# Expert loop of a two-block model: TensorE's order tied to the program, down products one expert later, return products two later

## The chip, the cores and the metric

The kernel runs on one core of one Trainium2 chip. The metric is the time of one execution on the device in microseconds; shown is the median of three runs. A profile of one further execution comes with it.

## What is computed

The program is a two-block model of 256 tokens with width 1024: a mixer and a memory attention, then a mixture of experts, then a second block of feed-forward parts, a recurrence and an attention. The change touches the mixture of experts alone. Each token goes to the two best of 32 experts, and an expert is a gated unit with three matrices:

```python
def hierarchical_moe(h, w_route_group, b_route_group, w_route_expert, b_route_expert,
                     w_gate, w_up, w_down):
    t = h.reshape(-1, D)                                  # 256 tokens x 1024
    ...                                                   # top-1 group, top-2 experts in it
    gates = jnp.sum(jax.nn.one_hot(ids, N_EXPERTS) * w[..., None], axis=1)
    gates = gates.astype(h.dtype).T                       # 32 x 256, two non-zero per token

    def expert_step(y, args):
        wg, wu, wd, ge = args                             # 1024x512, 1024x512, 512x1024
        out = (jax.nn.silu(t @ wg) * (t @ wu)) @ wd
        return y + ge[:, None] * out, None

    y, _ = lax.scan(expert_step, jnp.zeros_like(t), (w_gate, w_up, w_down, gates))
    return y.reshape(B, S, D)
```

All of it is in float32; the weights of the 32 experts are 192 MiB, and each is read once.

## The kernel before

An expert works on 64 slots (`CAP`) instead of 256 tokens. Eight steps belong to one expert e, in `experts` (L772) and its helpers:

- **Gather** (L807, matmuls at L815): a one-hot matrix `oh` brings the tokens' columns into slots, in two halves `tokh` and `tokl`. It is done for a group of four experts at a time, a quarter per expert, while the group before is worked on; the result goes from a PSUM bank of ring "B" into the tiles `gx`, two copies by VectorE (L821) and two by ScalarE (L819).
- **Slots** (L823): two matmuls turn `oh` around (L828), ScalarE copies the result to `oT` (L830); two more fetch the slots' gate and norm factor (L833), VectorE adds them to `gt` (L835). The two results stand in two banks of ring "B".
- **Gate/up product** (`expert_in`, L872, matmuls at L879): four weight tiles t = 0 to 3 of 1024 KB; gate and up stand in the upper and lower half of a bank of ring "A".
- **gu** (L856): ScalarE scales that bank into `gu`.
- **Transposes** (`expert_act`, L882, L887): four, into a bank of ring "A"; then `sl` by ScalarE (Silu, L889) and `hx` by VectorE (L891).
- **Down product** (`expert_down`, L894, L903): two weight tiles, into a bank of ring "B"; then `yh` by ScalarE (L906) and `yl` by VectorE (L907), high and low part of the gated result.
- **Return product** (`combine`, L910, L917): 16 matmuls take `yh` and `yl` with `oT` back to tokens and add them into four PSUM banks `acc` that stay for the whole loop.

A matmul here has 64 columns of output partitions in the gate/up and down products (two stand side by side in the array), 128 in the gather, slots and transposes, and 64 rows in the return product. A float32 matmul of a weight tile shows as two records in the trace, so a weight tile is 8 records.

In the program, iteration e writes: the first two gate/up tiles of e, the down product of e-1, the last two gate/up tiles of e, gu, a quarter of the next group's gather, the slots of e+1, the return product of e-1, the transposes and hx of e. The order on the engines is not that of the program: a scheduler places each engine's instructions by its own estimate of when they can start, so pieces move against each other. After expert 5 stands a branch (`rest`, L764 to L767) that all engines take: only if an expert had more than 64 tokens is its body run. The scheduler works on the part ahead of the branch and the part behind it separately.

Weight tiles are loaded by SyncE's queue (`wraw`, L160), in order, into 12 buffers: six named `raw`, three `wh`, three `wl`, taken in turn as wh, raw, wl, raw. A load waits until the tile twelve back has been used. The tiles of the last expert all go into `raw`, because `wh` and `wl` hold split weights of the next part, the feed-forward part (its tiles come from `ffn_w`, its splits are at L156 and L157, its matmuls at L171 to L173). PSUM rings "A" and "B" have two banks each, `acc` four.

Of the kernel before, what the change touches and what calls it, by code (L numbers as in the profile page):

```python
# [8 lines left out]
F32 = mybir.dt.float32  # L9
F32R = mybir.dt.float32r  # L10
# [3 lines left out]
AX = mybir.AxisListType  # L14
PSUM = bass.MemoryType.PSUM

P = 128
T = 256
D = 1024
# [3 lines left out]
NE = 32  # L23
CAP = 64
# [23 lines left out]
class Block:  # L48
    def __init__(s, ctx, tc, io):
        s.tc, s.nc, s.ctx, s.io = tc, tc.nc, ctx, io  # L50
        s.n = s.turn = s.place = 0
        pool = lambda name, bufs, **k: ctx.enter_context(tc.tile_pool(name=name, bufs=bufs, **k))
        s.cp = pool("const", 1)
        s.wp = pool("weights", 3)
        s.tp = pool("temps", 2)
        s.xp = pool("x", 1)
        s.pa = pool("acc", 1, space=PSUM)
        s.pp = pool("ps", 2, space=PSUM)
# [713 lines left out]
    def experts(s, mt, pos, gs, rest):  # L772
        nc = s.nc
        mm = nc.tensor.matmul

        num = s.new(mt, [P, CAP], "num")
        nc.gpsimd.iota(num, pattern=[[1, CAP]], base=1, channel_multiplier=0, allow_small_or_imprecise_dtypes=True)
        idr = s.new(mt, [P, P], "idr", F32R)
        nc.scalar.copy(idr, s.ident)


        hh, hl = s.pair(mt, 2, "tok", N=D)
        for k in range(0, KC, 2):
            pt = s.ps([P, 2, 2, P])
            for j in range(2):
                xs = s.tmp([P, T])
                nc.scalar.mul(xs, s.xT[:, k + j], s.col("norm_ffn_g", k + j))
                for h in range(2):
                    nc.tensor.transpose(pt[:, h, j], xs[:, h * P:(h + 1) * P], s.ident)
            dst = slice(k * P, (k + 2) * P)  # L790
            src = pt.rearrange("p h j b -> p h (j b)")
            nc.scalar.copy(hh[:, :, dst], src)
            nc.vector.tensor_sub(hl[:, :, dst], src, hh[:, :, dst].bitcast(F32))

        def group(e0):


            n = 4
            oh = s.new(mt, [P, 2, n, 2 * CAP], "oh", F32R, 2)
            sh = [P, n, 2, CAP]  # L800
            for h in range(2):
                nc.vector.tensor_tensor(oh[:, h].rearrange("p n (a c) -> p n a c", a=2),
                                        num.unsqueeze(1).unsqueeze(1).to_broadcast(sh),
                                        pos[:, h, e0:e0 + n].unsqueeze(2).unsqueeze(3).to_broadcast(sh), op=ALU.is_equal)
            return n, oh, ([], [])

        def gather(g, k):  # L807

            n, oh, gx = g
            if not gx[k // 4]:  # L810
                gx[k // 4].extend(s.new(mt, [P, 4, CAP], "gx", F32, 12) for _ in range(n))
            pg = s.ps([P, 2, n, CAP], "B")
            for j in range(2):
                for i, (src, h) in enumerate(((hh, 0), (hh, 1), (hl, 0), (hl, 1))):
                    mm(pg[:, j], src[:, h, (k + j) * P:(k + j + 1) * P], oh[:, h, :, 0:CAP], start=i == 0, stop=i == 3)  # L815
            for i, x in enumerate(gx[k // 4]):
                dst = x[:, k % 4:k % 4 + 2]
                if i % 2:
                    nc.scalar.copy(dst, pg[:, :, i])  # L819
                else:  # L820
                    nc.vector.tensor_copy(dst, pg[:, :, i])  # L821

        def slots(g, e, i):  # L823

            oh = g[1][:, :, i]
            pt = s.ps([P, 2, P], "B")
            for h in range(2):
                mm(pt[:, h], oh[:, h], idr, start=True, stop=True)  # L828
            oT = s.new(mt, [P, 2 * P], "oT", F32R, 3)
            nc.scalar.copy(oT, pt.rearrange("p a b -> p (a b)"))  # L830
            pg = s.ps([P, 2, 2], "B")
            for h in range(2):
                mm(pg.rearrange("p a b -> p (a b)"), oh[:, h], gs[:, h, e], start=h == 0, stop=h == 1)  # L833
            gt = s.new(mt, [P, 2], "gt", F32, 4)
            nc.vector.reduce_sum(gt, pg, axis=AX.X)  # L835
            return oT, gt

        nxt = group(0)
        for k in range(0, KC, 2):
            gather(nxt, k)  # L840
        prev = None
        acc = s.accs()
        for e in range(NE):
            i = e % 4
            if i == 0:
                now = nxt
                nxt = group(e + 4) if e + 4 < NE else None
                slot = slots(now, e, 0)
# [23 lines left out]
    def expert_in(s, ps, e, gx, part):  # L872


        for t in (2 * part, 2 * part + 1):
            w = s.wraw(s.io["w_gu"][e, t], 4, 512, e == NE - 1).rearrange("p (g c) n -> p g c n", c=2)
            for c in range(2):
                for g in range(2):
                    s.nc.tensor.matmul(ps[g * CAP:(g + 1) * CAP], gx[part][:, 2 * (t % 2) + c], w[:, g, c],  # L879
                                       start=t + c == 0, stop=t == 3 and c == 1)  # L880

    def expert_act(s, mt, gu):  # L882

        nc = s.nc
        pt = s.ps([P, 4, P], "A")
        for c in range(4):
            nc.tensor.transpose(pt[:, c], gu[:, c * P:(c + 1) * P], s.ident)  # L887
        sl = s.new(mt, [P, 4, CAP], "sl")
        nc.scalar.activation(sl, pt[:, :, 0:CAP], AF.Silu)  # L889
        hx = s.new(mt, [P, 4, CAP], "hx")  # L890
        nc.vector.tensor_mul(hx, sl, pt[:, :, CAP:P])  # L891
        return hx

    def expert_down(s, mt, e, hx, oT, gt):  # L894


        nc = s.nc
        pd = s.ps([P, 512], "B")
        for t in range(2):
            w = s.wraw(s.io["w_down"][e, t], 2, D, e == NE - 1)  # L900
            for c in range(2):
                for n in range(2):
                    nc.tensor.matmul(pd[n * CAP:(n + 1) * CAP], hx[:, 2 * t + c], w[:, c, n * 512:n * 512 + 512],  # L903
                                     start=t + c == 0, stop=t + c == 2)
        yh, yl = (s.new(mt, [P, 512], n, F32R) for n in ("yh", "yl"))
        nc.scalar.mul(yh, pd, gt[:, 0:1])  # L906
        nc.vector.scalar_tensor_tensor(yl, pd, gt[:, 0:1], yh.bitcast(F32), op0=ALU.mult, op1=ALU.subtract)  # L907
        return yh, yl

    def combine(s, acc, e, y, oT):  # L910

        mm = s.nc.tensor.matmul
        for m in range(KC // 2):
            for i in range(2):
                for n in range(2):
                    r, k = slice(n * CAP, (n + 1) * CAP), 4 * n + m
                    mm(acc[k // 2][:, k % 2], y[i][r, m * P:(m + 1) * P], oT[r], start=e == 0 and i == 0 and m % 2 == 0,  # L917
                       stop=e == NE - 1 and i == 1 and m % 2 == 1)

    def moe_over(s, over, y):  # L920

# [425 lines left out]
```

## Time and profile before

| | |
|---|---|
| median of three runs | 1767.74 us (1766.97 to 1768.96) |
| the profiled execution's own time | 1765.29 us |
| its span in the profile | 1763.5 us |
| TensorE busy, share of the span | 96% |
| expert loop, first gate/up matmul to last return matmul | 256.4 to 771.9 us |
| weight tiles of the experts | 192 of 1024 KB |

The profile shows one execution. PE is TensorE's matmuls, PEld its weight loads, DVE is VectorE, ACT ScalarE, SPq SyncE's queue. A busy TensorE in this table is not one at its peak: a group of matmuls that run side by side counts as busy throughout. Times inside the loop are in microseconds from the span's start.

### The profile page before, as it was taken

To read this page: it belongs to the slowest core of one execution; us is meant where nothing else is said; L and a number is where in the kernel's file an instruction comes from. 1 tells how busy PE (TensorE), PEld (TensorE's weight loads), DVE (VectorE), ACT (ScalarE), POOL (GpSimd) and SP (SyncE) were. 2 spreads that over 40 slices of the span, in tenths; PEclk is the share of its full clock that TensorE was granted. 3 is DMA by queue.
4 is the path that set the end of the run, shared out by engine and by line. 5 is a ranking of instruction groups with operands and counts; after the bars stand their busy time and mean duration, and the time that the engine had idled before them with its cause. 6 is when DMAs were issued, how large, how long until landed. Compare 5 with 4: busy or idle time off the path is not lost.

```text
span 1763.5 us, 28035 instructions
## 1 busy us (share of the span) xinstructions
PE 1690.5 (96%) x11820; PEld 1356.1 (77%) x11820; DVE 932.2 (53%) x1643; ACT 706.3 (40%) x1140; POOL 3.5 (0%) x19
## 2 busy tenths in 40 slices
PE   8999989999999999879999999999999999999998
PEld 7879974443333333359999999999899998689998
DVE  7998651111111111057556896555856557876554
ACT  8426432111111111144444774434644445864442
POOL 0000000000000000000000000000000000000000
PEclk9999989999999999989999999999999999899999
DMA  8425359999999999775554645555455555135540
GB/s 319 164 80 184 124 204 403 373 419 415 380 391 385 389 383 395 299 259 195 192 188 135 222 152 213 191 183 177 176 187 186 192 178 181 49 122 189 191 168 25
DMA packets 60225, 408.01 MB, mean 231 GB/s; under 512 B 6592, under 2 KB 9920, under 8 KB 11456
## 3 DMA queue, kind: packets, MB, share of 16 engines
q1 hardware_dynamic: 60096, 406.18, 62.1%
q8 instruction: 94, 1.54, 0.3%
q14 instruction: 35, 0.29, 0.0%
HBM read 405.11 MB, written 1.05 MB: 230 GB/s over the span
## 4 chain that ended last, share of the span: by engine, by line
PE 74%; ACT 3%; DVE 3%; issue 1%; ACTq 0%; DVEq 0%
PE A L879 11%; PE acc L172 6%; PE acc L171 6%; PE acc L173 6%; PE B L172 6%; PE B L171 6%; PE B L903 6%; PE B L173 5%; PE A L172 5%; PE A L173 5%; PE A L171 5%; PE acc L917 2%; PE B L815 1%; ACT yh L906 1%; ACT gu L856 1%; PE A L887 1%
## 5 line engine op out<-in xcount | busy, mean ns | idle before, releaser
L156 ACT CAST wh<-raw 128x1024 fp32r<-128x1024 f32 (+2 forms) x378 | 377.9, 1033 | 425.8 <-issue 368.7
L157 DVE TENSOR_TENSOR wl<-raw,wh 128x1024 fp32r<-128x1024 f32 (+2 forms) x378 | 448.9, 1204 | 145.3 <-ACT wh L156 144.3
L171 PE MATMUL B<-xgh,wh 128*128 128x256 f32 x872 | 246.2, 282 | 9.5 <-ACT wh L156 9.5
L171 PE MATMUL A<-xgh,wh 128*128 128x256 f32 (+1 forms) x872 | 246.0, 282 | 1.7 <-ACT xgh L215 1.7
L172 PE MATMUL A<-xgl,wh 128*128 128x256 f32 (+1 forms) x872 | 245.7, 282 | 0.3 <-DVE xgl L216 0.2
L172 PE MATMUL B<-xgl,wh 128*128 128x256 f32 x872 | 245.8, 282 | 0.0
L173 PE MATMUL B<-xgh,wl 128*128 128x256 f32 x872 | 245.6, 282 | 0.0
L173 PE MATMUL A<-xgh,wl 128*128 128x256 f32 (+1 forms) x872 | 244.9, 281 | 0.6 <-DVE wl L157 0.5
L172 PE MATMUL acc<-hl,wh 128*128 128x256 f32 x704 | 198.2, 283 | 0.2
L173 PE MATMUL acc<-hh,wl 128*128 128x256 f32 x704 | 198.2, 283 | 0.0
L171 PE MATMUL acc<-hh,wh 128*128 128x256 f32 x704 | 195.5, 282 | 0.1
L171 PEld LDWEIGHTS B<-xgh,wh 128*128 128x128 f32 x872 | 164.6, 189 | 10.7 <-ACT wh L156 10.1
L171 PEld LDWEIGHTS A<-xgh,wh 128*128 128x128 f32 (+1 forms) x872 | 164.4, 189 | 2.3 <-ACT xgh L215 1.9
L173 PEld LDWEIGHTS B<-xgh,wl 128*128 128x128 f32 x872 | 164.4, 189 | 1.5 <-DVE wl L157 1.0
L172 PEld LDWEIGHTS A<-xgl,wh 128*128 128x128 f32 (+1 forms) x872 | 164.3, 188 | 1.3 <-DVE xgl L216 1.2
L173 PEld LDWEIGHTS A<-xgh,wl 128*128 128x128 f32 (+1 forms) x872 | 164.2, 188 | 1.1 <-DVE wl L157 1.1
L172 PEld LDWEIGHTS B<-xgl,wh 128*128 128x128 f32 x872 | 164.7, 189 | 0.5 <-DVE xgl L216 0.2
L172 PEld LDWEIGHTS acc<-hl,wh 128*128 128x128 f32 x704 | 132.3, 188 | 0.6 <-DVE hl L213 0.6
L171 PEld LDWEIGHTS acc<-hh,wh 128*128 128x128 f32 x704 | 132.1, 189 | 0.8 <-ACT hh L212 0.7
L173 PEld LDWEIGHTS acc<-hh,wl 128*128 128x128 f32 x704 | 132.2, 188 | 0.0
L879 PE MATMUL A<-raw,gx 128*64 128x512 f32 x528 | 130.3, 598 | 0.0
L891 DVE TENSOR_TENSOR hx<-sl,A 128x256 f32<-128x256 f32 x32 | 13.5, 421 | 167.9 <-ACT sl L889 167.9
(404 smaller groups left out, 2449.6 us busy)
## 6 DMA issues: line engine op xcount, KB each, us to landing
raw<-in_ffn_w_dram SPq DMA_DIRECT2D x132, 1024.0 KB, 4.9
raw<-in_w_gu_dram SPq DMA_DIRECT2D x66, 1024.0 KB, 7.5
raw<-in_w_down_dram SPq DMA_DIRECT2D x33, 1024.0 KB, 8.3
wh<-in_w_gu_dram SPq DMA_DIRECT2D x31, 1024.0 KB, 7.3
wl<-in_w_gu_dram SPq DMA_DIRECT2D x31, 1024.0 KB, 7.1
wh<-in_w_down_dram SPq DMA_DIRECT2D x16, 1024.0 KB, 8.8
wl<-in_w_down_dram SPq DMA_DIRECT2D x15, 1024.0 KB, 8.9
raw<-in_a_w_in_dram SPq DMA_DIRECT2D x8, 1024.0 KB, 4.8
```

Of the source, the lines that this page charges most:

```text
L156: nc.scalar.copy(wh[:, lo:hi], raw[:, lo:hi])
L157: nc.vector.tensor_sub(wl[:, lo:hi], raw[:, lo:hi], wh[:, lo:hi].bitcast(F32))
L171: mm(out, w[0], x[0], start=first, stop=False)
L172: mm(out, w[0], x[1], start=False, stop=False)
L173: mm(out, w[1], x[0], start=False, stop=last)
L815: mm(pg[:, j], src[:, h, (k + j) * P:(k + j + 1) * P], oh[:, h, :, 0:CAP], start=i == 0, stop=i == 3)
L856: nc.scalar.mul(gu, ps, rs)
L879: s.nc.tensor.matmul(ps[g * CAP:(g + 1) * CAP], gx[part][:, 2 * (t % 2) + c], w[:, g, c], start=t + c == 0, stop=t == 3 and c == 1)
L887: nc.tensor.transpose(pt[:, c], gu[:, c * P:(c + 1) * P], s.ident)
L903: nc.tensor.matmul(pd[n * CAP:(n + 1) * CAP], hx[:, 2 * t + c], w[:, c, n * 512:n * 512 + 512], start=t + c == 0, stop=t + c == 2)
L906: nc.scalar.mul(yh, pd, gt[:, 0:1])
L917: mm(acc[k // 2][:, k % 2], y[i][r, m * P:(m + 1) * P], oT[r], start=e == 0 and i == 0 and m % 2 == 0, stop=e == NE - 1 and i == 1 and m % ...
```

## The change

TensorE's instructions in the expert loop get a fixed order: a new helper `pe` adds, from each matmul to the next one in the program, a dependency that costs no semaphore and binds the scheduler alone. It starts anew behind the branch. The program's order is rearranged: an iteration e now writes all four gate/up tiles of e, gu, the return product of e-2, a quarter of the gather, the slots of e+1, the transposes of e, and then the down product of e-1. The slots' two results share one bank, all four matmuls standing together. The down product's bank comes from ring "A" instead of "B"; `oT` gets four buffers instead of three, `hx` two instead of one. The first expert's slots come ahead of the loop; the last six weight tiles (two gate/up tiles of expert 31 and both down products of 30 and 31) go into `raw`.

```diff
+        slot = slots(nxt, 0, 0)
+        s.queue = []
+        prev = done = None
...
-            ps = s.ps([P, 512], "A")
-            s.expert_in(ps, e, gx, 0)
-            if prev is not None:
-                yy = s.expert_down(mt, *prev)
-            s.expert_in(ps, e, gx, 1)
+            ps = s.expert_in(e, gx)
             gu = s.new(mt, [P, 512], "gu", F32, 2)
             nc.scalar.mul(gu, ps, rs)
+            if done is not None:
+                s.combine(acc, *done)
             if nxt:
                 gather(nxt, 2 * i)
             own = slot
-            if i < 3 and e + 1 < NE:
-                slot = slots(now, e + 1, i + 1)
+            if e + 1 < NE:
+                slot = slots(nxt if i == 3 else now, e + 1, (i + 1) % 4)
+            hx = s.expert_act(mt, gu)
             if prev is not None:
-                s.combine(acc, e - 1, yy, prev[2])
-            hx = s.expert_act(mt, gu)
+                done = prev[0], s.expert_down(mt, *prev), prev[2]
             prev = (e, hx, *own)
             if e == 5:
                 rest()
-        yy = s.expert_down(mt, *prev)
-        s.combine(acc, NE - 1, yy, prev[2])
+                s.queue = []
+        last = prev[0], s.expert_down(mt, *prev), prev[2]
+        s.combine(acc, *done)
+        s.combine(acc, *last)
+        s.queue = None
...
+    def pe(s, ins):
+
+        if s.queue is not None:
+            if s.queue:
+                s.after(s.queue.pop(), ins)
+            s.queue.append(ins)
+        return ins
...
-        pd = s.ps([P, 512], "B")
+        pd = s.ps([P, 512], "A")
         for t in range(2):
-            w = s.wraw(s.io["w_down"][e, t], 2, D, e == NE - 1)
+            w = s.wraw(s.io["w_down"][e, t], 2, D, e >= NE - 2)
```

Every matmul of the loop is wrapped in `s.pe(...)`; `slots` puts its second result into columns 256 to 259 of the first one's bank.

TensorE in the steady loop behind the branch, expert 8, before. The names are output and inputs: `A<-wl,gx` is a gate/up tile, `B<-wh,hx` a down tile, `oh,tokh` a gather, `idr,oh` and `gs,oh` the slots, `acc<-oT,yh` a return matmul, `ident,gu` a transpose.

```order
L879 MATMUL A_3723<-wl_3724,gx_3139 64x512 x4
L879 MATMUL A_3723<-raw_3730,gx_3139 64x512 x4
L903 MATMUL B_3736<-wh_3737,hx_3708 64x512 x4
L815 MATMUL B_3771<-oh_3710,tokh_2623 128x256 x2
...
L903 MATMUL B_3736<-raw_3743,hx_3708 64x512 x4
L828 MATMUL B_3784<-idr_2621,oh_3082 128x128 x2
L917 MATMUL acc_2732<-oT_3596,yh_3749 128x256
...
L833 MATMUL B_3789<-gs_377_2611,oh_3082 128x4 x2
...
L879 MATMUL A_3723<-wl_3753,gx_3576 64x512 x4
L917 MATMUL acc_2732<-oT_3596,yl_3750 128x256
...
L879 MATMUL A_3723<-raw_3759,gx_3576 64x512 x4
L887 MATMUL A_3810<-ident,gu_3765 128x128 x4
```

And now, the same expert (the gate/up lines are L891, down L916, return L930, gather L816, slots L829 and L832, transposes L900):

```order
L891 MATMUL A_3698<-wl_3699,gx_3117 64x512 x4
L891 MATMUL A_3698<-raw_3705,gx_3117 64x512 x4
L891 MATMUL A_3698<-wh_3711,gx_3552 64x512 x4
L891 MATMUL A_3698<-raw_3717,gx_3552 64x512 x4
L930 MATMUL acc_2741<-oT_3230,yh_3691 128x256
...
L816 MATMUL B_3745<-oh_3695,tokh_2623 128x256 x2
...
L829 MATMUL B_3758<-idr_2621,oh_3071 128x128 x2
L832 MATMUL B_3758<-gs_377_2611,oh_3071 128x4 x2
L900 MATMUL A_3767<-ident,gu_3723 128x128 x4
L916 MATMUL A_3776<-wl_3777,hx_3676 64x512 x4
L916 MATMUL A_3776<-raw_3783,hx_3676 64x512 x4
```

Each kind of matmul stands in one piece; the return product stands between the gate/up product and the transposes, and the down tiles behind these.

SyncE's weight loads ahead of the branch, before:

```order
L165 DMA wl_3205<-in_w_down_dram 128x2048
L165 DMA raw_3211<-in_w_down_dram 128x2048
L165 DMA wh_3221<-in_w_gu_dram 128x2048
L165 DMA raw_3227<-in_w_gu_dram 128x2048
L165 DMA wl_3533<-in_w_gu_dram 128x2048
L165 DMA raw_3539<-in_w_gu_dram 128x2048
L165 DMA wh_3546<-in_w_down_dram 128x2048
L165 DMA raw_3552<-in_w_down_dram 128x2048
L767 COMPARE_AND_BRANCH
```

And now:

```order
L166 DMA wl_3182<-in_w_gu_dram 128x2048
L166 DMA raw_3188<-in_w_gu_dram 128x2048
L166 DMA wh_3244<-in_w_down_dram 128x2048
L166 DMA raw_3250<-in_w_down_dram 128x2048
L166 DMA wl_3510<-in_w_gu_dram 128x2048
L166 DMA raw_3516<-in_w_gu_dram 128x2048
L166 DMA wh_3522<-in_w_gu_dram 128x2048
L166 DMA raw_3528<-in_w_gu_dram 128x2048
L768 COMPARE_AND_BRANCH
```

38 loads stand ahead of the branch in both. The last four are those of iteration 6: two gate/up and two down tiles before, four gate/up tiles now.

## Rows read from the trace of the kernel before

**Rows 1.** The page, part 2: GB/s in 40 slices of 44 us.

```profile
GB/s 319 164 80 184 124 204 403 373 419 415 380 391 385 389 383 395 299 259 195 192 188 135 222 152 213 191 183 177 176 187 186 192 178 181 49 122 189 191 168 25
```

**Rows 2.** Stretches of the expert loop, with the columns' names ahead.

```profile
core 0: us, PE busy (x) PEld busy (x) DVE busy (x) ACT busy (x) POOL busy (x), PEclk, DMA share, GB/s
284.00:328.00 44.00, 43.52 (x255) 20.22 (x253) 6.86 (x17) 7.97 (x19) 0.00 (x0) 1.00 1.01 420
340.00:428.00 88.00, 79.35 (x427) 34.09 (x429) 12.72 (x32) 13.52 (x33) 0.00 (x0) 1.00 1.01 419
430.00:709.00 279.00, 257.18 (x1370) 107.85 (x1366) 36.19 (x91) 43.59 (x103) 0.00 (x0) 1.00 0.98 387
```

**Rows 3.** Waits, 250 to 790 us: who for whom, us, times, longest.

```profile
PE A L887 <- ACT gu L856: 19.7, 25, 0.8
PE acc L917 <- ACT yh L906: 14.0, 26, 0.8
PEld A L879 <- DMA raw<-in_w_down_dram: 0.9, 3, 0.3
SPq L165 <- PE A L879: 303.0, 116, 9.6
```

**Rows 4.** Timeline, one expert behind the branch: start, us, instruction, [idle before].

```profile
399.91 1.94 PE L903 MATMUL B<-raw,hx 128*64 128x512 f32 x8
...
402.69 0.50 PE L917 MATMUL acc<-oT,yh 64*128 64x256 f32 x3 [0.48 <-ACT yh L906]
...
409.25 0.66 PE L887 MATMUL A<-ident,gu 128*128 128x128 f32 x4 [0.79 <-ACT gu L856]
...
409.84 1.94 PE L879 MATMUL A<-wl,gx 128*64 128x512 f32 x8
...
410.42 0.42 DVE L891 TENSOR_TENSOR hx<-sl,A 128x256 f32<-128x256 f32 x1 [6.72 <-ACT sl L889]
...
416.28 1.94 PE L903 MATMUL B<-raw,hx 128*64 128x512 f32 x8
```

**Rows 5.** Timeline of TensorE, two experts ahead of the branch.

```profile
295.50 0.50 PE L815 MATMUL B<-oh,tokh 128*128 128x256 f32 x2
...
309.91 0.50 PE L815 MATMUL B<-oh,tokh 128*128 128x256 f32 x2
...
311.05 0.39 PE L917 MATMUL acc<-oT,yh 64*128 64x256 f32 x2
...
312.20 0.66 PE L887 MATMUL A<-ident,gu 128*128 128x128 f32 x4
...
313.13 1.94 PE L879 MATMUL A<-wl,gx 128*64 128x512 f32 x8
...
323.58 0.50 PE L815 MATMUL B<-oh,tokh 128*128 128x256 f32 x2
```

**Rows 6.** Timeline of SyncE's queue: weight loads at the refill and around the branch.

```profile
261.63 0.33 SPq L165 DMA_DIRECT2D wh<-in_w_down_dram  x1
...
272.57 0.33 SPq L165 DMA_DIRECT2D wh<-in_w_gu_dram  x1
...
320.26 0.33 SPq L165 DMA_DIRECT2D raw<-in_w_down_dram  x1
333.51 0.34 SPq L165 DMA_DIRECT2D wl<-in_w_gu_dram  x1
```

**Rows 7.** Stretches of 4 us around the branch, columns as in rows 2.

```profile
328.00:332.00 4.00, 4.00 (x22) 1.40 (x20) 0.42 (x1) 0.10 (x1) 0.00 (x0) 1.00 0.54 221
332.00:336.00 4.00, 4.00 (x22) 1.33 (x20) 0.54 (x1) 0.69 (x1) 0.00 (x0) 1.00 0.37 94
```

**Rows 8.** Timeline of TensorE at the end of the loop.

```profile
765.64 3.65 PE L903 MATMUL B<-raw,hx 128*64 128x512 f32 x16 [0.93 <-DVE hx L891]
...
771.58 0.28 PE L917 MATMUL acc<-oT,yl 64*128 64x256 f32 x2
773.54 0.58 PE L171 MATMUL A<-xgh,wh 128*128 128x256 f32 x1 [1.69 <-ACT xgh L215]
```

More of the change, by code (lines that the diff above doesn't have):

```diff
@@ L814, in gather @@
                 for i, (src, h) in enumerate(((hh, 0), (hh, 1), (hl, 0), (hl, 1))):
[L815 removed]
+                    s.pe(mm(pg[:, j], src[:, h, (k + j) * P:(k + j + 1) * P], oh[:, h, :, 0:CAP], start=i == 0, stop=i == 3))
             for i, x in enumerate(gx[k // 4]):
@@ L825, in slots @@
             oh = g[1][:, :, i]
-            pt = s.ps([P, 2, P], "B")
+            pt = s.ps([P, 512], "B")
             for h in range(2):
[L828 to L831, printed above, removed]
+                s.pe(mm(pt[:, h * P:(h + 1) * P], oh[:, h], idr, start=True, stop=True))
+            pg = pt[:, T:T + 4]
             for h in range(2):
-                mm(pg.rearrange("p a b -> p (a b)"), oh[:, h], gs[:, h, e], start=h == 0, stop=h == 1)
+                s.pe(mm(pg, oh[:, h], gs[:, h, e], start=h == 0, stop=h == 1))
+            oT = s.new(mt, [P, 2 * P], "oT", F32R, 4)
+            nc.scalar.copy(oT, pt[:, 0:T])
             gt = s.new(mt, [P, 2], "gt", F32, 4)
-            nc.vector.reduce_sum(gt, pg, axis=AX.X)
+            nc.vector.reduce_sum(gt, pg.rearrange("p (a b) -> p a b", b=2), axis=AX.X)
             return oT, gt
@@ L847, in experts @@
                 nxt = group(e + 4) if e + 4 < NE else None
-                slot = slots(now, e, 0)
             gx, rs = [x[i] for x in now[2]], slot[1][:, 1:2]
-            ps = s.ps([P, 512], "A")
-            s.expert_in(ps, e, gx, 0)
-            if prev is not None:
-                yy = s.expert_down(mt, *prev)
-            s.expert_in(ps, e, gx, 1)
+            ps = s.expert_in(e, gx)
             gu = s.new(mt, [P, 512], "gu", F32, 2)
             nc.scalar.mul(gu, ps, rs)
+            if done is not None:
+                s.combine(acc, *done)
             if nxt:
@@ L867, in experts, with expert_in @@
                 rest()
-        yy = s.expert_down(mt, *prev)
-        s.combine(acc, NE - 1, yy, prev[2])
-        return acc
-    def expert_in(s, ps, e, gx, part):
-        for t in (2 * part, 2 * part + 1):
-            w = s.wraw(s.io["w_gu"][e, t], 4, 512, e == NE - 1).rearrange("p (g c) n -> p g c n", c=2)
+                s.queue = []
+        last = prev[0], s.expert_down(mt, *prev), prev[2]
+        s.combine(acc, *done)
+        s.combine(acc, *last)
+        s.queue = None
+        return acc
+    def pe(s, ins):
[4 more added lines that the diff above has]
+        return ins
+    def expert_in(s, e, gx):
+        ps = s.ps([P, 512], "A")
+        for t in range(4):
+            w = s.wraw(s.io["w_gu"][e, t], 4, 512, e == NE - 1 and t > 1).rearrange("p (g c) n -> p g c n", c=2)
             for c in range(2):
                 for g in range(2):
-                    s.nc.tensor.matmul(ps[g * CAP:(g + 1) * CAP], gx[part][:, 2 * (t % 2) + c], w[:, g, c],
-                                       start=t + c == 0, stop=t == 3 and c == 1)
+                    s.pe(s.nc.tensor.matmul(ps[g * CAP:(g + 1) * CAP], gx[t // 2][:, 2 * (t % 2) + c], w[:, g, c],
+                                            start=t + c == 0, stop=t == 3 and c == 1))
+        return ps
     def expert_act(s, mt, gu):
@@ L897, in expert_down @@
         nc = s.nc
-        pd = s.ps([P, 512], "B")
+        pd = s.ps([P, 512], "A")
         for t in range(2):
-            w = s.wraw(s.io["w_down"][e, t], 2, D, e == NE - 1)
+            w = s.wraw(s.io["w_down"][e, t], 2, D, e >= NE - 2)
             for c in range(2):
                 for n in range(2):
-                    nc.tensor.matmul(pd[n * CAP:(n + 1) * CAP], hx[:, 2 * t + c], w[:, c, n * 512:n * 512 + 512],
-                                     start=t + c == 0, stop=t + c == 2)
+                    s.pe(nc.tensor.matmul(pd[n * CAP:(n + 1) * CAP], hx[:, 2 * t + c], w[:, c, n * 512:n * 512 + 512],
+                                          start=t + c == 0, stop=t + c == 2))
         yh, yl = (s.new(mt, [P, 512], n, F32R) for n in ("yh", "yl"))
@@ L916, in combine @@
                     r, k = slice(n * CAP, (n + 1) * CAP), 4 * n + m
-                    mm(acc[k // 2][:, k % 2], y[i][r, m * P:(m + 1) * P], oT[r], start=e == 0 and i == 0 and m % 2 == 0,
-                       stop=e == NE - 1 and i == 1 and m % 2 == 1)
+                    s.pe(mm(acc[k // 2][:, k % 2], y[i][r, m * P:(m + 1) * P], oT[r],
+                            start=e == 0 and i == 0 and m % 2 == 0, stop=e == NE - 1 and i == 1 and m % 2 == 1))
     def moe_over(s, over, y):
```

5 lines of the change are left out of this document (2 added, 3 removed).

## Prediction

> **What bounds the kernel now.** I read the slices of the page first, to find the stretch: from about 265 to 750 us the moved data stand at 180 to 420 GB/s, far above the 170 to 220 of most other slices [rows 1]. That stretch is the expert loop. Everything outside it is left alone by the change, so only this stretch is worth reading closely. Second come stretches of the loop, with what DMA moved. Two levels are to be seen [rows 2]: 420 and 419 GB/s in 284 to 328 and 340 to 428 us, with the DMA share at 1.01, and 387 GB/s from 430 to 709 us. Third, the waits show which side gives way [rows 3]. TensorE waited for a weight tile only 3 times, 0.9 us in all, while SyncE's queue stood 303.0 us waiting for TensorE to leave a buffer. So at 387 GB/s DMA is paced by TensorE: TensorE's own order is the bound, and 419 to 420 is what DMA does when buffers are free.
>
> Then one expert after the branch, row by row [rows 4]. From the second down tile of one expert (399.91) to that of the next (416.28) are 16.37 us. Inside it TensorE stands 0.48 us until ScalarE has written yh from the down product that has just ended, and 0.79 us until ScalarE has moved the gate/up product into gu. The view of waits has these 26 and 25 times [rows 3], so most of the 32 experts pass like this. Last, an expert before the branch, where the same code got another order [rows 5]: 295.50 to 309.91 is 14.41 us, 309.91 to 323.58 is 13.67 us, and the latter row by row has no wait: gather at 309.91, return products at 311.05, transposes at 312.20, then slots, six weight tiles from 313.13 to 323.58. So the same matmuls take 13.67 us when each kind stands in one piece and 16.37 when they are interleaved. Of the 2.70 us, 1.27 are the two waits; the other 1.43 I put down to changes between kinds of matmul (11 in the one, 5 in the other), an inference.
>
> **The change, part by part.** *Down one expert later, return products two later, order tied.* The steady order becomes four gate/up tiles, 16 return matmuls of expert e-2, 8 gather matmuls, 4 slot matmuls, 4 transposes, 2 down tiles of e-1. It issues the same matmuls as [rows 5] in as few pieces, so TensorE's need per expert is 13.67 us, up to 14.41 if something like the oT wait of the neighbour expert came back. I take 13.8, next to the row whose pieces are the same.
>
> Each of today's waits gets a cover. gu: ScalarE needs 0.7 us and the way there and back, and 16 return and 8 gather matmuls (1.15 us from 311.05, 1.14 us from 309.91 [rows 5], 2.3 together) stand between. yh and yl: a whole gate/up block of 4 tiles, about 6.9 us (10.45 x 4/6 [rows 5]), stands between down and its return products. hx: it is used an expert later. The slots' two parts share one PSUM bank and are issued together, so TensorE no longer waits for the copy oT between them. Each cover gone would cost what [rows 4] show, 0.5 to 0.8 us an expert.
>
> *The PSUM ring "A"* gets three tiles an expert instead of two, of two buffers: the next gate/up product takes the bank that the transposes filled, and so waits for hx. After the transposes (409.25) hx starts at 410.42 and takes 0.42 us [rows 4], 1.6 us in all; the slots' oT copy and a gx copy may stand ahead of it on ScalarE, so up to 2.5. The down tiles between are 3.5 us. Price zero, with about 1 us to spare.
>
> *The weight queue on SyncE* asks for tiles in exactly TensorE's order (four gate/up, two down). Twelve buffers stay twelve, and tile k still waits for tile k-12. The four extra tiles ahead of the branch stay four.
>
> *So what is late next is DMA.* An expert needs 6 tiles of 1024 KB, 6.29 MB; at 419.5 GB/s that is 15.0 us, 2.50 a tile. TensorE at 13.8 gains 1.2 us an expert on DMA, uses up its lead of some six tiles by about the middle of the loop, and from there on waits for every tile. The end is set by the last tile's landing. Its sum: twelve tiles land ahead of the loop; the refill starts with the issue at 261.63 [rows 6], at full rate 1.6 us later (after the issue at 333.51 [rows 6] the row 332 to 336 [rows 7] holds 94 GB/s x 4 us = 0.9 us of full rate, so it began at 335.1), at 263.2. 180 tiles x 2.50 = 450.0 us. Two holes: after the first four refills (10 us, to 273.2) the next was issued at 272.57 before and comes about 0.5 us later with the change, 1.5 us lost. At the branch SyncE issues nothing for 13.25 us (320.26 to 333.51). That cost about 5.0 us of DMA time before: the row 328 to 332 at 221 GB/s [rows 7] ends the stream at 330.1, and it resumes at 335.1. The last issue ahead of it waits for tile 25, which with the change is expert 4's last gate/up tile instead of expert 3's second down tile; by the pieces of [rows 5] it is done near 316.7, 3.4 us sooner, so the stream, ending near 329.7, resumes at 331.6: 1.9 us lost, at worst 5.0. Landing of the last tile: 263.2 + 450.0 + 1.5 + 1.9 = 716.6 us.
>
> Behind it: the tile's matmuls, 1.7 us, then what stands behind the last down product before, from 769.1 (765.64 + 2 tiles of 1.74, 10.45 / 6 [rows 5]) to 771.86 [rows 8], 2.76 us, in which the return products of expert 30 hide except for 0.1. The loop ends at 721.1 instead of 771.86: 50.8 us less. TensorE's own path without any DMA wait is the check: resuming at about 340.3 after the branch, 26 experts x 13.8 + two down tiles and the end (6.2) = 705, below 721; it becomes the bound above 14.4 us an expert, then 2.6 us for each 0.1.
>
> *The feed-forward part behind* needs its first tile when ScalarE is done with yh; those tiles follow the last expert tile at 2.5 us steps (719.1, 721.6), and TensorE started 1.7 us after the loop's end before [rows 8]. Its price is 0 to 2 us; I take 0.
>
> The profiled execution took 1765.29 us (span 1763.5), 2.45 below the median of the runs, 1767.74. 1765.29 - 50.8 = 1714.5, by the median **1717 us**.
>
> A page speaks against this. What the rows show is 419 to 420 GB/s over 44 and 88 us on end [rows 2]. The Trainium skill, "DMA: Bandwidth & Descriptors", section "Where 436 GB/s comes from", says that for HBM to SBUF the HBM side binds at about 358 GB/s per core. By that rule an expert could not be fed in under 17.6 us, an estimate from the page, and the change would end later than before (rival 3); the rows are above it for 132 us. The same page has 425 GB/s measured for a 16 MB transfer by a core alone, and the trace agrees with that.
>
> **The rivals.** (1) *A wait comes back on TensorE.* With a tied order nothing fills a wait, so something like the 0.79 or 0.48 us of [rows 4], or the changes between kinds, stays: 14.6 to 15.8 us an expert, 726 to 757 us for the end, 1722 to 1753 us in all; the middle, 15.1, gives 1735. For it: the order has no slack by design. Against: every producer has over 2 us of cover. (2) *DMA falls to the rate of the long stretch*, 387 GB/s: there the DMA share reads 0.98 [rows 2], as though nearly full. 2.71 us a tile, 38 us more: 1755. Against: that stretch is paced by SyncE's waits [rows 3]. (3) *Slower*: with up to twelve tiles always outstanding over 380 us, a load pattern that lasted 88 us at most before, DMA settles below what TensorE took from it. The place is the stretch after the branch; the price is 1.8 us for each 0.01 us a tile, and it decides at 2.78 us a tile (716.6 + 180 x 0.28 + 4.5 = 771.5), 377 GB/s. At 370 GB/s, 2.83 us a tile, the loop would end at 781 and the time be 1777. Against: the rate did not sag within the 88 us. The Trainium skill's section named above would have it happen; at its 358 GB/s the same sum, an estimate, gives 1794. (4) *It doesn't do what it says*: the tie orders the scheduler's work alone and could be outvoted; the order of the changed kernel shows the pieces as written after the branch, so only no gain by balance of (1) or (2) is left, 1767.
>
> **How the numbers follow.** Forecast (DMA-bound, 1709 to 1726 by 1% of the rate and the holes) 0.74. Rival (1) 0.11, (2) 0.07, (3) 0.05, (4) 0.03. The range reaches from 1709 through the nearer half of (1): to 1738, which leaves out about 0.18. What tells from no change here is about 0.2%, 3.5 us. Faster 0.92, same 0.03, slower 0.05.
>
> **What would show it.** Right: experts after the branch at 13.7 to 14 us at first, then at 15.0 with waits of TensorE's weight loads on DMA; 415 to 420 GB/s and a DMA share of 1.0 from 340 us to the loop's end; no waits on gu or yh; the last return product near 721. Wrong in the order: waits on gu, yh or hx, and pace over 14.4 with DMA under 410. Wrong in the rate: waits on tiles at under 410 GB/s. If the feed-forward part is starved, its first matmul comes later than 1.7 us behind the loop.

## The result, and the profile after

The changed kernel takes 1720.82 us (median of four runs, 1719.17 to 1721.33); the kernel before, with a fourth run beside the three that were shown, 1768.35 (1766.97 to 1771.55). The ratio is 0.9727, 95% interval 0.971 to 0.9744. The profiled execution of the changed kernel took 1721.14 us, its span is 1719.4.

What moved is the loop, and its bound. First the page's data rate in 40 slices (43 us each), against [rows 1]:

```profile
GB/s 315 180 74 196 117 206 357 377 419 419 419 419 419 419 419 419 420 213 196 196 178 117 224 195 195 190 181 145 215 181 193 178 190 172 50 123 178 190 172 26
```

From the ninth slice to the seventeenth it stands at 419 to 420; before, it held 419 and 415 for two slices and then 380 to 395. Stretches of the loop, against [rows 2] (the same columns):

```profile
340.00:428.00 88.00, 88.00 (x506) 39.64 (x504) 13.65 (x34) 14.89 (x36) 0.00 (x0) 0.99 1.01 419
430.00:660.00 230.00, 215.13 (x1230) 92.84 (x1230) 33.04 (x85) 38.20 (x94) 0.00 (x0) 1.00 1.01 419
660.00:716.00 56.00, 50.32 (x275) 18.40 (x270) 4.75 (x10) 7.77 (x14) 0.00 (x0) 1.00 1.01 420
```

TensorE is busy without a break from 340 to 428 us and then has gaps, while DMA has none. The waits of the loop, against [rows 3] (in total, times, longest):

```profile
PEld A L891 <- DMA raw<-in_w_gu_dram: 41.9, 40, 1.4
PE A L891 <- DMA raw<-in_w_gu_dram: 13.0, 24, 0.6
PEld A L891 <- DMA wh<-in_w_gu_dram: 11.6, 9, 1.4
```

The waits for gu are gone, that for yh is left once, at the loop's end. TensorE and its weight loads now wait for tiles. An expert early in the stretch behind the branch and one late in it, by their transposes (start, duration), against [rows 4]:

```profile
350.00 0.66 PE L900 MATMUL A<-ident,gu 128*128 128x128 f32 x4
350.58 1.94 PE L916 MATMUL A<-wl,hx 128*64 128x512 f32 x8
...
363.59 0.66 PE L900 MATMUL A<-ident,gu 128*128 128x128 f32 x4
```

```profile
501.90 1.94 PE L891 MATMUL A<-raw,gx 128*64 128x512 f32 x8 [0.55 <-DMA raw<-in_w_gu_dram]
...
506.33 0.66 PE L900 MATMUL A<-ident,gu 128*128 128x128 f32 x4
...
514.40 1.94 PE L891 MATMUL A<-wh,gx 128*64 128x512 f32 x8 [0.40 <-DMA wh<-in_w_gu_dram]
516.89 1.51 PE L891 MATMUL A<-raw,gx 128*64 128x512 f32 x6 [0.56 <-DMA raw<-in_w_gu_dram]
```

The first is 13.59 us and has no wait: TensorE's own need. Of the second the next transposes start at 521.34, 15.01 us later, and the gate/up tiles follow each other at 2.49 us (514.40 to 516.89): the pace of the tiles. The first wait for a tile behind the branch:

```profile
439.56 1.94 PE L891 MATMUL A<-wl,gx 128*64 128x512 f32 x8 [0.33 <-DMA wl<-in_w_gu_dram]
```

The end, against [rows 8], on TensorE, ScalarE and VectorE:

```profile
722.93 1.94 PE L916 MATMUL A<-raw,hx 128*64 128x512 f32 x8 [0.47 <-DMA raw<-in_w_down_dram]
...
727.12 0.38 PE L930 MATMUL acc<-oT,yh 64*128 64x256 f32 x2 [1.11 <-ACT yh L919]
728.45 0.58 PE L930 MATMUL acc<-oT,yl 64*128 64x256 f32 x2 [0.95 <-DVE yl L920]
...
729.90 0.41 PE L930 MATMUL acc<-oT,yl 64*128 64x256 f32 x2
731.76 0.58 PE L172 MATMUL A<-xgh,wh 128*128 128x256 f32 x1 [1.45 <-ACT xgh L216]
```

```profile
725.43 1.05 ACT L157 CAST wh<-raw 128x1024 fp32r<-128x1024 f32 x1 [4.50 <-DMA raw<-in_ffn_w_dram]
726.38 0.68 ACT L919 ACTIVATE yh<-A,gt 128x512 fp32r<-128x512 f32 x1
```

```profile
726.51 1.23 DVE L158 TENSOR_TENSOR wl<-raw,wh 128x1024 fp32r<-128x1024 f32 x1 [4.79 <-DMA raw<-in_ffn_w_dram]
727.65 0.74 DVE L920 SCALAR_TENSOR_TENSOR yl<-A,gt,yh 128x512 fp32r<-128x512 f32 x1
```

The loop ends at 730.3 (729.90 + 0.41) instead of 771.86, 41.6 us earlier. What stands behind the loop took 991.6 us before (1763.5 - 771.86) and takes 989.1 now, 2.5 less. Together that is the 44.1 us between the two spans.

### The profile page after: what moved, and what is told of

Same layout as the page of the kernel before. It is cut to its first block, busy times and chain, and to the rows that moved or that the text cites. A ratio compares the mean times of both kernels' runs of the same rounds, so it can differ in the third digit from the quotient of the medians.

```text
span 1719.4 us, 28024 instructions
## 1 busy us (share of the span) xinstructions
PE 1664.9 (97%) x11820; PEld 1350.0 (79%) x11820; DVE 931.3 (54%) x1643; ACT 704.3 (41%) x1140; POOL 3.5 (0%) x19
## 4 chain that ended last, share of the span: by engine, by line
PE 61%; DMA 16%; DVE 3%; ACT 1%; issue 0%; DVEq 0%; SPq 0%; ACTq 0%
DMA raw<-in_w_gu_dram 14%; PE acc L173 6%; PE acc L172 6%; PE acc L174 6%; PE B L173 6%; PE B L172 6%; PE B L174 6%; PE A L173 6%; PE A L174 6%; PE A L172 5%; PE A L891 3%; PE A L916 1%; DMA raw<-in_w_down_dram 1%; DVE wl L158 1%; PE acc L930 1%; PE B L816 1%
## 5 line engine op out<-in xcount | busy, mean ns | idle before, releaser
L822 DVE COPY gx<-B 128x128 f32<-128x128 f32 x64 | 18.6, 291 | 247.3 <-PE B L816 239.0
L891 PE MATMUL A<-raw,gx 128*64 128x512 f32 x520 | 126.0, 597 | 13.0 <-DMA raw<-in_w_gu_dram 13.0
```

The source lines that it names most:

```text
L891: s.pe(s.nc.tensor.matmul(ps[g * CAP:(g + 1) * CAP], gx[t // 2][:, 2 * (t % 2) + c], w[:, g, c], start=t + c == 0, stop=t == 3 and c == 1))
```

## The experiments

Each ratio is to the kernel before as it ran in the same comparison (medians 1766.79, 1768.08 and 1769.05 us in the three). The traces are of single executions, and the loop's first matmul does not start at the same time in all of them: at 256.5 us in the changed kernel's, at 260.0 to 264.7 in `tie_only` and the two with the branch ahead, at 254.2 to 259.1 in the others. Where a landing time or a loop's end is compared, this has to be taken off.

### Tie alone, rearrangement alone

The first is the kernel before with every matmul of its loop tied, as in this line and six like it, with the queue begun ahead of the loop and behind the branch:

```diff
-                mm(pt[:, h], oh[:, h], idr, start=True, stop=True)
+                s.pe(mm(pt[:, h], oh[:, h], idr, start=True, stop=True))
```

> Only the tie is added to the kernel before; its program order, its banks and its buffers stay. TensorE's order is then, for every expert: two gate/up tiles of e, two down tiles of e-1, two gate/up tiles of e, gather, slots, 16 return products of e-1, transposes of e. Theory D (DMA is the bound once each kind stands in one piece): yh has two gate/up tiles and a gather ahead of its use (4.6 us), hx two gate/up tiles (3.5 us), gu gather, slots and return products (2.9 us), so TensorE needs 14 to 14.5 us an expert, below the 15.0 of the tiles, and the time is that of the changed kernel, 1717 to 1726. Rival R (the rearrangement takes the waits away, the tie alone leaves some, of banks above all, since gather, both parts of the slots and down share the two banks of ring B): 15.1 to 15.9 us an expert, 1728 to 1750.

1721.83 us (1720.14 to 1722.90), ratio 0.9737 (0.9718 to 0.9757): the tie alone gives all of it. Theory D holds. One expert of it:

```profile
546.99 0.66 PE L899 MATMUL A<-ident,gu 128*128 128x128 f32 x4
...
560.54 0.38 PE L834 MATMUL B<-gs,oh 128*128 128x4 f32 x2 [0.78 <-ACT oT L831]
...
562.00 0.66 PE L899 MATMUL A<-ident,gu 128*128 128x128 f32 x4
```

R's bank is there, a wait of 0.78 us for the slots' copy in two of three experts, but the mean expert of this order is 14.42 us (four in a row: 14.68, 14.68, 13.33, 15.01), and that is still below the tiles' 15.0: the tiles land at the usual step of 2.49 us from the refill on, the branch and a few jumps apart, and the last at 723.90.

The second is the changed kernel without the tie:

```diff
-        s.queue = []
         prev = done = None
...
                 rest()
-                s.queue = []
```

> The changed kernel without the tie: the program stays rearranged and the scheduler orders TensorE again. It puts the first return products right behind the down product, the transposes right behind the gate/up product and cuts the slots and the return products in two, 9 to 11 pieces an expert. Theory D: the waits of 0.48 us for yh and 0.79 us for gu come back and with them the changes between kinds, 15.3 to 16.2 us an expert: 1733 to 1757. Rival (the tie does nothing that the rearranged program doesn't do by itself): 1717 to 1726.

1758.23 us (1755.71 to 1759.86), ratio 0.9942 (0.9921 to 0.9963): theory D, one microsecond above its range. The waits are back, in nearly every expert behind the branch:

```profile
PE acc L928 <- ACT yh L917: 19.2, 23, 0.8
PE A L898 <- ACT gu L853: 18.9, 24, 0.8
```

Experts take 15.75 and 16.84 us in turn, 16.30 on average. Of the 2.71 above 13.59 the two waits are 1.64 (0.85 and 0.79); 1.07 are left, and I put them down to some five more changes between kinds of matmul, about 0.2 each; no run isolates that.

### Is DMA the bound?

```diff
-            for j in range(2):
+            for j in (0, 1) if s.queue is None else (0, 0, 1, 1):
                 for i, (src, h) in enumerate(((hh, 0), (hh, 1), (hl, 0), (hl, 1))):
```

> The changed kernel with each gather product of the loop computed twice over into the same bank: 8 more matmuls an expert for the first 28 experts, 1.14 us each time by the row of the kernel before. Theory D: 13.7 + 1.14 = 14.8 us is still below the 14.96 us that six tiles take, so the work goes into TensorE's waits for tiles: 0 to 4 us more, 1721 to 1725. Rival T (TensorE's own pace sets the end): 28 x 1.14 = 32 us more, 1753.

1720.91 us (1719.85 to 1722.31): 0.96 us more an expert (14.55 in place of 13.59 early in the loop), 27 us in all, cost nothing. Rival T is out. It only just fits: of TensorE's waits for tiles none is left between 345 and 700 us, only the one at the branch:

```profile
PE A L891 <- PEq L768: 4.2, 1, 4.2
```

The other way, an expert with one tile less to load:

```diff
-        for t in range(2):
-            w = s.wraw(s.io["w_down"][e, t], 2, D, e >= NE - 2)
+        w = s.wraw(s.io["w_down"][e, 0], 2, D, e >= NE - 2)
+        for t in range(2):
```

> The changed kernel with five tiles loaded for an expert instead of six: the second down tile is left out and the first used in its place, so the down product is not the reference's; TensorE's instructions are the same. Theory D: five tiles take 12.5 us, TensorE's own 13.7 to 13.9 us becomes the bound, no waits for tiles are left, the loop ends at 700 to 712 and the time is 1692 to 1704. The pace per expert then shows TensorE's need by itself. Rival T (TensorE's own pace sets the end): no change, 1719 to 1723.

1685.07 us (1683.67 to 1689.84), 36 us less than `gather_twice` beside it with the changed kernel's instructions on TensorE, and 7 below the range I gave, in part since I reckoned with 13.7 to 13.9 us an expert:

```profile
502.01 0.66 PE L900 MATMUL A<-ident,gu 128*128 128x128 f32 x4
...
515.61 0.66 PE L900 MATMUL A<-ident,gu 128*128 128x128 f32 x4
```

It is 13.60, and stays so for every expert behind the branch that has a gather. The traced execution is the longest of the four (1689.84); its loop runs from 259.1 to 699.4, 33.5 us shorter than the changed kernel's. So 13.6 us is TensorE's need, and the tiles keep 33 to 36 us of what the order would allow.

The second pass of the gather in the kernel before, by the same edit of its loop (`busy` is false for the first group, ahead of the loop):

```diff
-            for j in range(2):
+            for j in (0, 0, 1, 1) if busy else (0, 1):
```

> The kernel before with each gather product of the loop computed twice over, as it was done in the changed kernel. Theory (TensorE's own order was the bound before): the 0.96 us an expert that the second pass cost TensorE in the changed kernel, 28 times, comes on top: 27 us, 1790 to 1800. Rival (the 387 GB/s of the long stretch was already what DMA could give): 1766 to 1772.

1776.87 us (1776.22 to 1783.33), ratio 1.0059 (1.0037 to 1.0081): neither range was met. The order isn't tied here, so the scheduler placed everything anew and put the second pass where TensorE had stood waiting (in total, times, longest, 345 to 750 us):

```profile
PE A L887 <- ACT gu L856: 7.8, 21, 0.8
...
PE acc L917 <- ACT yh L906: 5.1, 21, 0.8
```

The kernel before has 18.9 and 12.4 us for the same two in this stretch (the whole loop is in [rows 3]), so 18.4 of the 27 us went into waits. That the time rose, with TensorE still waiting for no tile, speaks for TensorE as the bound before; as a measure of it the run is spoilt.

### The hole at the branch

```diff
-            if e == 5:
+            if e == 20:
```

> The changed kernel with the branch behind expert 20 instead of expert 5. Theory D (DMA is the bound; the branch costs what DMA stands empty, since SyncE's queue is silent for 16.0 us while only some 13 us of transfers are outstanding at expert 5): by expert 20 the lead is used up, eight tiles of 2.5 us are outstanding (20 us from issue to landing), so the silence is covered, and the 2.9 to 4.1 us of the hole go: last tile 3 to 4 us earlier, 1716 to 1719. Rival (the silence grows with what is outstanding, since the code for the branch has to come through the same engines; the hole stays as it is or TensorE's own stall at the branch takes its place): 1720 to 1724.

1719.25 us (1718.12 to 1722.68), between the two ranges. The trace decides for the rival. SyncE's queue at the branch, and what DMA moved:

```profile
531.76 0.33 SPq L166 DMA_DIRECT2D raw<-in_w_gu_dram  x1
552.80 0.34 SPq L166 DMA_DIRECT2D wl<-in_w_gu_dram  x1
```

```profile
548.00:550.00 2.00, 2.00 (x12) 0.61 (x10) 0.34 (x1) 0.04 (x1) 0.00 (x0) 1.00 0.63 254
550.00:552.00 2.00, 0.99 (x6) 0.11 (x2) 0.18 (x1) 0.69 (x1) 0.00 (x0) 1.00 0.15 61
552.00:554.00 2.00, 0.85 (x4) 0.40 (x6) 0.57 (x1) 0.00 (x0) 0.00 (x0) 1.00 0.49 70
```

The silence grew from 16.0 to 21.0 us with what was outstanding, and DMA ran empty all the same: the step between two tiles is 6.26 us at the hole. The reason I gave (code that comes through the same engines) isn't needed: behind the compare (316.67 in the changed kernel, 532.14 here) the trace has on SyncE a wait on each of the eight semaphores of its loads. In the changed kernel the first ends at 329.21, the second, that of the last load, at 331.69, the others at once, and the next load is issued at 332.26. So SyncE waits, where the branch's two ways meet again, until its loads have landed.

The other way, the branch out of the loop:

```diff
         acc = s.accs()
+        rest()
+        s.queue = []
         for e in range(NE):
...
-            if e == 5:
-                rest()
-                s.queue = []
```

> The changed kernel with the branch ahead of the loop: exactly the twelve loads that fit the buffers stand ahead of it on SyncE. Theory (behind the compare SyncE waits for every load that is outstanding, so a branch costs the stream one emptying and refilling, 4 us, wherever it falls while DMA is busy): here it falls into the stretch from 253 to 262 us in which DMA stands empty anyway; TensorE's own stall at the branch, some 2 us, shifts the loop's start, and the 4.1 us of the hole go: 1717 to 1720, and no second hole in the loop. Rival (TensorE's, ScalarE's and VectorE's stalls at the loop's start add up to as much): 1720 to 1724.

1723.95 us (1722.33 to 1724.29): the rival holds. There is no second hole, but TensorE pays at the start:

```profile
264.53 3.45 PE L890 MATMUL A<-wh,gx 128*64 128x512 f32 x8 [3.93 <-PEq L768]
```

It starts 8 us later than the changed kernel's 256.5. Of these 3.9 are the idle stretch at the branch (TensorE's own compare lasts 3.31 us in it, for a reason that stays open); in the rest the gather and the slots run, which now all stand ahead of the first gate/up tile. The refill begins at 268.00 instead of 261.77, and the last tile lands at 724.3 instead of 722.9.

### The end, and more buffers

yh and yl of the last expert are kept in `ends`, and the next weights' casts are tied behind them:

```diff
-            nc.scalar.copy(wh[:, lo:hi], raw[:, lo:hi])
-            nc.vector.tensor_sub(wl[:, lo:hi], raw[:, lo:hi], wh[:, lo:hi].bitcast(F32))
+            a = nc.scalar.copy(wh[:, lo:hi], raw[:, lo:hi])
+            b = nc.vector.tensor_sub(wl[:, lo:hi], raw[:, lo:hi], wh[:, lo:hi].bitcast(F32))
+            if ends:
+                s.after(ends[0], a)
+                s.after(ends[1], b)
```

> The changed kernel with the feed-forward part's first two casts on ScalarE and the two subtractions on VectorE tied behind yh and yl of expert 31. In the changed kernel one cast of 1.05 us and one subtraction of 1.23 us stand ahead of them. Theory E (the end behind the last tile is on the path that sets the time): yh starts 1.4 us earlier, yl follows at once, the loop ends 2.0 us earlier and the time is 1.5 to 2.5 us less: 1718 to 1719.5. Rival (the feed-forward part waits for its casts or tiles anyway): 1720 to 1722.

1722.17 us (1720.86 to 1723.86): the rival holds. The loop does end 2.5 us earlier (727.56 + 0.28), but the feed-forward part gives it back, in part because its casts come later:

```profile
734.47 0.58 PE L178 MATMUL A<-xgh,wl 128*128 128x256 f32 x1 [0.62 <-DVE wl L159]
741.80 0.39 PE L176 MATMUL B<-xgh,wh 128*128 128x256 f32 x1 [0.79 <-ACT wh L158]
```

In the changed kernel neither wait is there. The two make 1.4 us of the 3.3 that are given back; 1.2 more are lost between its 17th and its 42nd matmul: these start 1.5 us earlier here, but the granted clock rises from its lower level no earlier (738 to 740 us reads 0.74, and 0.94 in the changed kernel). In the kernel before, TensorE waited 2.93 us for that cast, behind its first feed-forward matmuls.

```diff
-            gu = s.new(mt, [P, 512], "gu", F32, 2)
+            gu = s.new(mt, [P, 512], "gu", F32, 1)
...
-RAW, WHL = 6, 3
+RAW, WHL = 7, 3
```

> The changed kernel with seven raw buffers instead of six (gu has one buffer instead of two to make room). Theory D: DMA stands empty from 253 to 262 us, when all twelve buffers are full and TensorE has freed none; with a thirteenth, one tile of 2.5 us is taken out of the stream behind it, and the loop ends 2.5 us earlier: 1717 to 1719.5. Rival (a longer lead is given back, or the end is set elsewhere): 1720 to 1723.

1718.51 us (1715.76 to 1720.11), ratio 0.9719 (0.9704 to 0.9734): inside theory D's range, but not told apart from the changed kernel (0.971 to 0.9744) by the times. In the trace, that of the shortest execution, the last tile landed at 718.4, 4.5 us earlier; its loop began 2.4 us earlier, so about the one tile is left.

The edits of `raw7`, `casts_behind` and `branch20` in one kernel:

> The three edits together: branch behind expert 20, casts behind yh and yl, seven raw buffers. Theory D and E: the gains add, 6.5 to 9 us: 1712 to 1715. Rival (they overlap): 1716 to 1721.

1719.40 us (1717.29 to 1722.41): the rival holds, the gains don't add. The hole at the branch is still there (the step between two tiles is 6.0 us at 557), and the feed-forward part takes back what the end gains, as in `casts_behind`: the loop ends at 725.8, and 991.8 us stand behind it. What the buffer gives can't be told from noise here.

A fourteenth buffer, on top of the seventh `raw` (the rest of the edit makes room for it, as the expectation says):

```diff
-        s.place = 0 if last else (s.place + 1) % 4
-        tag, bufs = (("raw", RAW), ("wh", WHL), ("raw", RAW), ("wl", WHL))[s.place]
-        w = s.new(s.wp, [P, 2048], tag, F32, bufs).rearrange("p (c n) -> p c n", n=N)
+        s.place += 1
+        tag = "raw" if last else (["wh", "raw", "wl", "raw"] * 3 + ["raw", "rawx"] * (s.me is not None))[(s.place - 1) % (14 if s.me else 12)]
+        pool, bufs = {"raw": (s.wp, RAW), "wh": (s.wp, WHL), "wl": (s.wp, WHL), "rawx": (s.me, 1)}[tag]
+        w = s.new(pool, [P, 2048], tag, F32, bufs).rearrange("p (c n) -> p c n", n=N)
```

> The changed kernel with fourteen weight buffers in the expert loop instead of twelve: seven raw and one more of the loop's own (gu gets one buffer instead of two, and the body of the branch, which is not run with these inputs, shares its tiles to make room). Theory D: each further buffer takes 2.5 us out of the empty stretch ahead of the loop; with one the last tile landed 4.5 us earlier (2.5 expected, the rest from the engines' spread), with two 5 us: 1714 to 1718. Rival (the gain of one buffer was chance, or the feed-forward part takes it back): 1719 to 1722.

1714.28 us (1712.52 to 1719.15), ratio 0.9698 (0.968 to 0.9715), inside theory D's range and the lowest of all kernels that load every tile; the last tile lands at 715.6. Ahead of the loop, the changed kernel first, then this one:

```profile
250.00:254.00 4.00, 4.00 (x20) 3.89 (x20) 3.24 (x9) 1.23 (x3) 0.00 (x0) 0.50 0.61 254
254.00:262.00 8.00, 8.00 (x42) 5.35 (x40) 3.58 (x11) 2.14 (x9) 0.00 (x0) 0.82 0.00 0
```

```profile
250.00:254.00 4.00, 4.00 (x21) 3.91 (x20) 3.67 (x10) 1.17 (x2) 0.00 (x0) 0.50 0.96 399
254.00:262.00 8.00, 8.00 (x44) 4.88 (x45) 2.94 (x10) 2.50 (x9) 0.00 (x0) 0.93 0.12 20
```

The changed kernel has its twelve tiles at 253.30 us, and nothing moves until after the issue at 261.77; here the fourteenth lands at 255.26 and the refill's first load is issued at 260.44. Of the 7.3 us by which the last tile lands earlier, 5.0 are the two tiles (2 x 2.49) and 1.1 the earlier refill (its first tile lands at 265.50, not 266.60), which is no gain of the buffers: the loop began 1.1 us earlier in this execution. The two kernels stand in different comparisons; set beside the changed kernel's 1720.82 (intervals of the ratios: 0.971 to 0.9744 and 0.968 to 0.9715) the difference is 0.3% and the intervals still touch, but its place is seen.

This with `branch_ahead`:

> Fourteen buffers and the branch ahead of the loop together. Theory: the gains add, 5 and 2 us, 1711 to 1716. Rival (they share the same empty stretch): no better than fourteen buffers alone.

1716.65 us (1715.37 to 1720.18): the rival holds, no better than fourteen buffers alone. The loop starts at 264.65, as in `branch_ahead`, and the last tile lands at 718.6.

## Why the prediction was right, point by point

**TensorE's order was the bound before.** Right: with the order tied and nothing else (`tie_only`) 45 us are gained, and the rearranged program in the scheduler's order (`untied`) gains 9.

**TensorE's need, 13.8 us an expert.** 13.59. Every cover held (gu, hx, yh, yl, the ring): up to the loop's end there is no wait but for tiles and the one of 2.15 us at the branch. The 1.43 us that were put down to changes between kinds stay an inference: in `untied` 1.07 us go with about five more changes, but nothing was run that changes their number alone.

**DMA becomes the bound.** Right, and shown from both sides: 27 us more of TensorE's work for nothing, a sixth of the tiles less for 33 to 36 us. The rate is 419 GB/s, the pace 15.0 us. The forecast's bound for TensorE, 14.4 us an expert, fits too: `tie_only` at 14.42 hardly waits for a tile. The lead was used up earlier than forecast: the first wait stands at 439.56, some 180 us into a loop of 474.

**The last tile at 716.6.** It landed at 722.9; this sum was 6.3 us short. Two terms were mis-sized. The landing events in the trace give each load's 16 shares apart. Here are the first and the last share of some tiles of the changed kernel (k counts from 0; usual step 2.49 us):

```
  k   issued   first share   last share   step of the last
 12   261.77      266.14        266.60      13.31
 13   264.18      268.64        270.55       3.95
 16   271.49      276.82        279.26       3.67
 38   332.26      336.68        337.09       5.41
 39   332.71      339.16        340.73       3.64
 66   388.29      406.53        409.59       3.91
141   576.88      593.80        598.16       3.83
191   709.95      718.39        722.88       2.50
```

The *hole at the branch* was put at 1.9 us and is 4.1 (5.41 + 3.64 - 2 x 2.49). The step that failed is "3.4 us sooner, so the stream, ending near 329.7, resumes at 331.6", which carries SyncE's resuming forward with its last issue: that issue came at 316.29 (316.7 forecast), but SyncE's silence was 15.97 us and not the 13.25 of before, since it lasts until the loads have landed. The 5.0 us "at worst" was the better number, and behind expert 20 the hole is hardly smaller (3.8 us, by a step of 6.26).

*The rate of the slowest of 16.* The sum took 2.50 us a tile for all. The usual step is 2.49, but a tile is complete when its last share is, and that fell back: the distance from first to last share is 0.46 us at tile 12 and 4.49 at the end. The last share comes 1.2 to 1.5 us late at tiles 13, 16, 39, 66 and 141, and this is made up only at the hole (0.41 us at tile 38). The sum had 1.5 us for the early stretch, for a load issued late behind the first four refills; that load was not late (tile 16 is issued at 271.49, 273.1 was reckoned), and the jumps outside the branch come to 5.4 (3.95 + 3.67 + 3.91 + 3.83 - 4 x 2.49). What remains of the 6.3 (2.2 + 3.9 = 6.1) is rounding: a first landing 0.9 later than reckoned, the step of 2.492 instead of 2.50, 1.4 less over 179 tiles, and 0.7 of small steps.

**4.5 us behind the last tile.** 7.4. The step "what stands behind the last down product before" left out that the feed-forward tiles now come right behind the last expert tile: a cast goes ahead of yh and a subtraction ahead of yl. yh starts at 726.38 instead of 724.9, when the last down product ends. The last return matmuls, behind TensorE's two idle stretches of 1.11 and 0.95 us, also fall into a stretch at 1.2 GHz (granted clock 0.50 from 728 us), 0.21 us a pair instead of 0.12.

**The feed-forward part, price 0 to 2, taken 0.** It gained 2.5 us, a sign I hadn't allowed: those early casts spare it the wait of 2.9 us for its first weights. `casts_behind` shows both ends of the trade; by its time nothing is gained or lost.

**The total.** 716.6 and 4.5 made 721.1; it was 730.3, 9.2 us later, and the feed-forward part gave 2.5 back. So the profiled execution took 1721.1 us where the sum said 1714.5, and the median is 1720.8 against 1717. That the loop's miss of 9.2 us shows as 4 in the median is luck: 2.5 went by this gain, and 2.8 because the profiled execution of the kernel before lay 2.45 under its median and that of the changed kernel 0.3 over its own.

**The rivals.** (1) didn't come: no such wait is left in the loop. `untied` has them, at 16.3 us an expert. (4) didn't come either: the order stands as written. (2) and (3), a lower rate of DMA under constant load, didn't come: 419 to 420 GB/s from 340 to 716 us, 376 us on end. The Trainium skill, "Perfetto Trace Analysis", section "Roofline", says that a lone core can draw more than its 358 GB/s share of HBM and is bounded by its 16 DMA engines at about 435 GB/s. The trace agrees: 419 to 420 lies between the two.

## What to carry to other kernels

Where a scheduler orders an engine that is the bound, look at what its order costs in waits before moving work: tying the engine to the order in which the program already had the work was enough here, and the rearrangement on top was worth nothing measurable. When a wait goes, work out the next bound as a stream from its first byte to its last: its empty stretches then go into the sum whole, and each buffer more took about one tile (2.5 us) out of the stream. The branch made SyncE wait until every load that it had issued had landed; it cost the stream one emptying behind expert 5 and behind expert 20 alike, and ahead of the loop it cost no less, at TensorE's start.

## What the runs showed of the hardware that was not expected

- The 16 shares of a load drift apart under constant load, to 2.31 us at tile 37 and, after the hole, from 0.41 to 4.49 us at the last tile, and come together only where the stream runs dry: in `branch20` 1.94 us are left at the end, behind a hole at 552 us, in place of 4.49. The Trainium skill, "DMA: Bandwidth & Descriptors", section "Why a DMA increments its semaphore by 16 and not by 1", says that the engines of a load finish independently and only the full count means that all has landed; the trace agrees, with that spread. A likely cause of the jumps are the 16 KB packets of instructions, which the profile counts on the same engines. The transfers of 590 to 600 us, around the jump at tile 141:

```profile
q1 hardware_dynamic: 568, 4.14, 100.2%
q8 instruction: 1, 0.02, 0.7%
```

  0.7% of 16 engines' 10 us is 1.1 us of one engine, near the jump of 1.3. In the changed kernel and the nine others here that load every tile in a tied order there are 28 jumps of 0.7 to 1.6 us from tile 20 on, not on the same tiles in all; each of the 28 has such a packet that starts 2.1 to 4.3 us ahead of the last share's landing, though the packets come some 22 us apart. The 22 packets in the loop make few jumps, so a jump would need the packet on the engine that is last already. Not all early jumps fit (none at tile 16), and no run took the packets away: the cause is likely, not shown.
- An idle stretch of 2.15 us on TensorE at the branch (its next matmul starts at 338.72) was followed by some 3.4 us at 1.2 GHz: the granted clock reads 0.86 and 0.72 in the two rows around it, and a gate/up tile took 3.32 us (338.72 to 342.04) instead of 1.72.

```profile
336.00:340.00 4.00, 1.85 (x8) 0.54 (x6) 0.75 (x1) 0.69 (x1) 0.00 (x0) 0.86 1.01 412
340.00:344.00 4.00, 4.00 (x16) 1.54 (x14) 0.00 (x0) 0.00 (x0) 0.00 (x0) 0.72 1.01 424
```

  It cost nothing, because TensorE had time to spare behind it.
